# Stick-breaking attention on TensorE: an order written down and pinned, with units of a pair of heads between steps of the next pairs' projections

## The chip, the cores and the metric

The kernel runs on one core of one Trainium2 chip. The metric is device time in microseconds (us) of one execution. The engines named here are TensorE (PE, matrix products and transposes; PEld are its weight loads), VectorE (DVE), ScalarE (ACT), GpSimd (POOL) and SyncE (SP), whose queue issues the transfers between buffers.

## The reference, cut to what matters

A 512 x 1024 input goes through a first block (sparse attention and retention) and a second one: a feed-forward layer, a hybrid mixer, cross attention to a memory, a second feed-forward layer. All values are 32-bit floats. The change lies in the mixer's stick-breaking attention, of 16 heads of 64:

```python
proj = u @ w_in
q, k, v, z, xs, bm, cm, dt_raw = jnp.split(proj, np.cumsum(IN_SPLITS)[:-1], axis=-1)
...
for i in range(s_ // SB_BLOCK):                    # blocks of 128 rows
    z = jnp.einsum('bhtd,bhsd->bhts', qb, kb) * scale
    causal = s_idx[None, :] < t_idx[:, None]
    log_1mb = jnp.where(causal, jax.nn.log_sigmoid(-z), 0.0)
    suffix = lax.cumsum(log_1mb, axis=3, reverse=True) - log_1mb
    log_a = jnp.where(causal, jax.nn.log_sigmoid(z) + suffix, -jnp.inf)
    a = jnp.exp(log_a)
    outs.append(jnp.einsum('bhts,bhsd->bhtd', a, vb.astype(jnp.float32)))
```

With l = sigmoid(-z) and E the running product of l from the right, a weight is the difference of two neighbouring E, so the sum over a times v is a sum over E times the differences of neighbouring rows of v. That is the form in which the kernel computes it.

## The kernel before, in words

**Products.** A product of float32 is made of three in a faster format: each operand is split into a high part (ACT copies it) and a low part (DVE subtracts). A projection of 128 columns (`proj_T`, matmuls on line 164) takes 8 chunks of the 1024 inputs with 3 matmuls each, 24 in all, with 512 rows moving through. Its weights arrive by a transfer (`raw`, line 99) and are split into `whi` and `wlo` (lines 82 and 83).

**Pairs of heads.** The loop `for p in range(8)` takes two heads at a time, e = 0 and 1. Of each pair it projects q (24 matmuls), then k (24). The results are split into qh, ql and kh, kl, and SP copies them into the tiles Q, K0 and K1 (lines 1056 and 1059) that hold, for each head, the operand twice, one above the other, so that one matmul against K0 (high part of k) and one against K1 (low part) give the score in full precision. The copies of K are eight transfers of 64 rows: high and low part, upper and lower half (r), each for e = 0 and 1. Head e needs the two halves of K0 and of K1.

**Units.** A pair has three units (`GROUPS`): row blocks 0 and 1 together, row block 2, row block 3. For each unit and head there are scores (line 1070), their sigmoid `l` on ACT (line 1074), a running product `E` on DVE from right to left (`TENSOR_TENSOR_SCAN`, line 1079), transposes of E on PE (line 1087), and copies of them into `aT`: by ACT for e = 0, by DVE for e = 1 (lines 1094 and 1096). The values (line 1027) multiply `aT` by the differences `vv`; they are put off (`held`) by one unit, so the values of unit 0 stand behind the transposes of unit 1, and those of unit 2 behind the transposes of unit 0 of the next pair. Scores lie in two PSUM banks of the pool `s` and every third in bank 2 (`mm` in the trace); projections take banks 0 and 1; the transposes of e = 1 take bank 3 (`mm`), those of e = 0 the pool `tp`.

**Differences of v.** `vbefore` (lines 956 to 968) is v moved down by one row; DMAs fill it from `vv`, and DVE subtracts (line 967). Two buffers are taken in turn, so the DMAs of the third and fourth row block wait for the first and second subtraction. Behind it stand the projections of z, whose four PSUM banks per half are read by ACT and DVE (`ev_z`, lines 972 to 983).

**Order.** The program is written pair after pair, and a scheduler decides the order of the instructions on each engine by priorities and by costs of its own. On PE it mixes projections of the next pairs with units of this one. `after` adds waits by hand: the first transpose of a unit, and the first matmul of the values, wait for the last scan of that unit. What is marked by `tc.keep_in_program_order` is not reordered among what is marked; SP, ACT and DVE stay with the scheduler.

Of the kernel before, what the change touches and what calls it, by code (L numbers as in the profile page):

```python
# [18 lines left out]
NT = 4  # L19
# [12 lines left out]
def block_kernel(ctx, tc, A, out, upto=99):  # L32
# [161 lines left out]
    def proj_X(src, c0, w, get, consume, K=8, nt=NT, tail=1, kp=2, korder=None, between=None, slots=(), ready=None):  # L194

        banks = [bank() for _ in range(nt)]
        nch = (K + kp - 1) // kp
        ko = korder or list(range(K))

        def mms(t, ch, hl):  # L200
            for k in range(kp):
                kk = ch * kp + k
                if kk >= K:
                    continue
                xh, xl = get(ko[kk], t, t + 1)
                xh, xl = xh[:, 0, :], xl[:, 0, :]
                wh, wl = hl[0][:, k, :], hl[1][:, k, :]
                for n, (a, b) in enumerate(((xh, wh), (xl, wh), (xh, wl))):
                    PE.matmul(banks[t][:, :w], a, b, start=(kk == 0 and n == 0), stop=(kk == K - 1 and n == 2))  # L209
                    tick(w)  # L210
        for ch in range(nch - tail):
            hl = wload(src, ko[ch * kp], min(kp, K - ch * kp), c0, w)
            for t in range(nt):
                mms(t, ch, hl)
            if between:
                between(ch)
        slots = (None,) * (tail - len(slots)) + tuple(slots)
        last = ready or [(ch, wload(src, ko[ch * kp], min(kp, K - ch * kp), c0, w, slots[ch - nch])) for ch in range(nch - tail, nch)]
        for t in range(nt):
            for ch, hl in last:  # L220
                mms(t, ch, hl)
            consume(t, banks[t][:, :w])
        if between:
            between(nch - 1)
# [544 lines left out]
    def mixer(pair, st):  # L769
# [183 lines left out]
            return f  # L953
        for c in range(2):
            proj_X(w, 2048 + c * 512, 512, get, ev_v(c))
        vbefore = lambda t: d1.tile([128, D], F32, name="vbefore", tag=("xdt", "xdec")[t % 2])
        vb = vbefore(0)
        V.memset(vb[0:1], 0.0)
        for t in range(NT):
            nc.sync.dma_start(vb[1:113], vv[0:112, t])  # L960
            nc.sync.dma_start(vb[113:128], vv[112:127, t])
            nxt = None
            if t < NT - 1:
                nc.sync.dma_start(vl[t * 8 + 8:t * 8 + 16], vv[127:128, t].rearrange("o (p c) -> o p c", p=8))
                nxt = vbefore(t + 1)
                nc.sync.dma_start(nxt[0:1], vv[127:128, t])
            V.tensor_tensor(vv[:, t], vb, vv[:, t], op=ALU.subtract)
            vb = nxt


        zs = l1.tile([128, NT, D], F32, name="zs", tag="u3")
# [15 lines left out]
            return t[:, 0], t[:, 1]  # L987
        for g in range(2):
            proj_X(w, 3072 + g * 512, 512, get, ev_z(g), tail=2, slots=[spare])
        tp = tpp.tile([128, 4, 128], F32, name="tp")  # L990
        PE.transpose(tp[:, 0, 0:32], vl, ident[0:32, 0:32])
        vlT = l1.tile([128, NT, 8], F32, name="vlT")
# [24 lines left out]
        def values(p, segs, aTs, ob):  # L1017


            def f(*others):  # L1020

                pv = [(0, 0, 2, 0), (1, 1, 1, 2)] if len(segs) == 2 else [(segs[0][0], j, 1, j) for j in range(segs[0][0] + 1)]
                first = True
                for i, j, n, o in pv:
                    for e in range(2):
                        h = 2 * p + e
                        m = PE.matmul(ob[64 * e:64 * e + 64, i * 128:(i + n) * 128], vv[:, j, h * 64:(h + 1) * 64], aTs[e][:, o:o + n],  # L1027
                                      start=(i == 0), stop=(n == 2 or j == i), skip_group_check=True)
                        if first:
                            after(m, *others)  # L1030
                            first = False
                if segs is GROUPS[-1]:
                    for i in range(NT):
                        sl = slice(i * 128, (i + 1) * 128)
                        ACT.activation(oaF[:, p, sl], ob[:, sl], AF.Identity, bias=vlT[:, i, p:p + 1])
                    if p == 0:
                        ACT.activation(sq, oaF[:, p], AF.Square)
                    else:
                        q2 = a1.tile([128, 512], F32, name="q2")
                        ACT.activation(q2, oaF[:, p], AF.Square)  # L1040
                        V.tensor_tensor(sq, sq, q2, op=ALU.add)
            return f

        for p in range(8):

            Q = qk.tile([128, 2, 512], F32R, name="Q")
            K = [qk.tile([128, 2, 512], F32R, name=f"K{i}") for i in range(2)]
            for nm, c0, scale in (("q", 0, 0.125), ("k", 1024, None)):
                hi = a1.tile([128, 512], F32R, name=f"{nm}h")
                lo = a1.tile([128, 512], F32R, name=f"{nm}l")  # L1050
                proj_T(w, c0 + p * 128, 128, get, lambda j, bank, hi=hi, lo=lo, sc=scale: split(hi, lo, bank, sc), of=(0, 1))
                for r in range(2):
                    for e in range(2):
                        rows = slice(64 * e, 64 * e + 64)
                        if nm == "q":
                            nc.sync.dma_start(Q[64 * r:64 * r + 64, e].bitcast(F32), (hi, lo)[r][rows].bitcast(F32))
                        else:
                            for i, x in enumerate((hi, lo)):
                                nc.sync.dma_start(K[i][64 * r:64 * r + 64, e].bitcast(F32), x[rows].bitcast(F32))
            ob = None  # L1060
            for segs in GROUPS:
                T = segs[-1][1] + (segs[-1][0] + 1) * 128
                css, last = [], None
                for e in range(2):
                    sb = score_bank(p)
                    first = True
                    for i, off in segs:
                        W = (i + 1) * 128
                        for n, k in enumerate(K):
                            PE.matmul(sb[:, off:off + W], Q[:, e, i * 128:(i + 1) * 128], k[:, e, :W], start=first, stop=(n == 1),  # L1070
                                      skip_group_check=True)
                            first = False
                    l = a2.tile([128, 512], F32, name="l", bufs=3)
                    ACT.activation(l[:, :T], sb[:, :T], AF.Sigmoid, scale=-1.0)  # L1074

                    E = a2.tile([128, 512], F32, name="E", bufs=5)
                    for off, W in (((0, 128), (128, 256)) if len(segs) == 2 else ((0, T),)):
                        rev = slice(off + W - 1, (off - 1) if off else None, -1)
                        last = V.tensor_tensor_scan(E[:, rev], l[:, rev], own1[:, 511:(511 - W) if W < 512 else None:-1], 1.0,  # L1079
                                                    op0=ALU.mult, op1=ALU.max)  # L1080
                    css.append(E)

                aTs = []
                for e in range(2):
                    tp = tpp.tile([128, 4, 128], F32, name="tp") if e == 0 or p == 7 else bank((3,)).rearrange("p (j q) -> p j q", j=4)
                    for j in range(T // 128):
                        m = PE.transpose(tp[:, j], css[e][:, j * 128:(j + 1) * 128], ident)
                        if e + j == 0:
                            after(m, last)
                    aT = a2.tile([128, 4, 128], F32, name="aT", bufs=4)  # L1090

                    n = T // 128
                    own, rest = (slice(0, 3, 2), slice(1, 2)) if len(segs) == 2 else (slice(n - 1, n), slice(0, n - 1))
                    (V.tensor_copy if e else ACT.copy)(aT[:, rest], tp[:, rest])
                    if e:
                        V.tensor_scalar(aT[:, own], tp[:, own], -1.0, None, op0=ALU.add)
                    else:
                        ACT.activation(aT[:, own], tp[:, own], AF.Identity, bias=less1)
                    aTs.append(aT)
                if held:  # L1100
                    held.pop()(last)
                if ob is None:
                    ob = op_.tile([128, 512], F32, name="ob")
                held.append(values(p, segs, aTs, ob))
        held.pop()()
        osT = new_act()
        for t in range(NT):
# [199 lines left out]
```

## Time and profile before

| | |
|---|---|
| time, median of 3 runs | 1955.26 us (1954.87 to 1957.7) |
| profiled execution: time, span | 1953.41 us, 1951.6 us |
| PE busy | 1903.7 us, 98% |
| PEld busy | 1556.5 us, 80% |
| DVE busy | 982.8 us, 50% |
| ACT busy | 721.8 us, 37% |
| granted clock of TensorE, mean | 0.997 of full speed |

The span is the time from the first to the last instruction of the profiled execution, and all starts below are counted from its beginning. The stretch that the change touches runs from about 1133 us (first projection of q and k) to about 1313 us. Before it, from about 1095 us, v is shifted and z is projected. A row of the time line gives start, length, engine, line, operation, what is written from what is read, and in brackets how long the engine stood idle before and what ended that. Matmuls overlap: the next starts before the one before has ended.

### The profile page before, as it was taken

Reading aid. Unit: us, or ns where it says so; the run is one execution under the profiler, and the core shown is the slowest. Engines: PE = TensorE matmul, PEld = TensorE weight load, DVE = VectorE, ACT = ScalarE, POOL = GpSimd, SP = SyncE. Lnnn points to the kernel's source line nnn. Section 1 sums busy time; section 2 is a strip of 40 time slices with the busy share of each in tenths; the row PEclk is TensorE's granted clock in tenths of the full one; section 3 lists DMA queues with packets and bytes.
Section 4 is the critical chain, followed back from the end, with each engine's and each line's share of the span. In section 5 each row is a group of like instructions: output and inputs, shape, how many; then the busy total and the mean of one; then the engine's idle time right before and its main releaser. Section 6 shows DMA issues by size and latency. Waiting matters only on the chain.

```text
span 1951.6 us, 24228 instructions
## 1 busy us (share of the span) xinstructions
PE 1903.7 (98%) x9677; PEld 1556.5 (80%) x9677; DVE 982.8 (50%) x1681; ACT 721.8 (37%) x1246; POOL 38.3 (2%) x66
## 2 busy tenths in 40 slices
PE   7999999999999999999999999999999999999998
PEld 6778888788878888888877877767788888888887
DVE  5578833724553333324668755665464553333223
ACT  4345533233333323223445434544353432323221
POOL 0000000100000000000000000000000000000000
PEclk9999999999999999999999999999999999999999
DMA  7411133232332333333321445442262312333322
GB/s 245 130 44 34 34 97 97 87 98 86 108 97 87 98 97 97 98 97 119 89 82 50 128 121 136 128 120 76 87 194 78 105 57 86 97 98 97 97 97 86
DMA packets 154336, 193.21 MB, mean 99 GB/s; under 512 B 9976, under 2 KB 111732, under 8 KB 154096
## 3 DMA queue, kind: packets, MB, share of 16 engines
q1 hardware_dynamic: 154224, 191.66, 32.7%
q8 instruction: 76, 1.25, 0.3%
q14 instruction: 36, 0.29, 0.0%
HBM read 174.85 MB, written 2.10 MB: 91 GB/s over the span
## 4 chain that ended last, share of the span: by engine, by line
PE 84%; DVE 8%; ACT 1%; issue 1%; POOL 1%; DMA 1%; POOLq 0%; DVEq 0%; ACTq 0%
PE mm L164 43%; PE mm L209 27%; PE mm L187 3%; DVE E L1079 1%; DVE x_sb L279 1%; POOL rp_r L76 1%; PE ob L538 1%; DVE h L251 1%; PE ob L1027 1%; PE s L561 1%; PE ob L924 1%; PE s L1182 1%; PE s L1070 1%; DVE fg L272 1%; PE mm L579 1%
## 5 line engine op out<-in xcount | busy, mean ns | idle before, releaser
L83 DVE TENSOR_TENSOR wlo<-raw,whi 128x1024 fp32r<-128x1024 f32 (+1 forms) x274 | 333.6, 1218 | 680.3 <-ACT whi L82 675.0
L82 ACT ACTIVATE whi<-raw 128x1024 fp32r<-128x1024 f32 (+1 forms) x274 | 289.0, 1055 | 687.3 <-PE mm L164 289.9
L164 PE MATMUL mm<-a_hi,wlo 128*128 128x512 f32 x1120 | 438.0, 391 | 1.6 <-DVE wlo L83 1.6
L164 PE MATMUL mm<-a_hi,whi 128*128 128x512 f32 x1120 | 438.9, 392 | 0.0
L164 PE MATMUL mm<-a_lo,whi 128*128 128x512 f32 x1120 | 438.5, 392 | 0.0
L164 PEld LDWEIGHTS mm<-a_hi,wlo 128*128 128x128 f32 x1120 | 210.3, 188 | 44.5 <-DVE wlo L83 2.0
L164 PEld LDWEIGHTS mm<-a_lo,whi 128*128 128x128 f32 x1120 | 210.3, 188 | 44.0 <-issue 2.4
L164 PEld LDWEIGHTS mm<-a_hi,whi 128*128 128x128 f32 x1120 | 210.3, 188 | 43.3 <-issue 1.4
L209 PE MATMUL mm<-whi,a_hi 128*128 128x512 f32 (+1 forms) x384 | 151.2, 394 | 2.3 <-ACT a_hi L82 2.3
L209 PE MATMUL mm<-whi,a_lo 128*128 128x512 f32 (+1 forms) x384 | 151.7, 395 | 0.0
L209 PE MATMUL mm<-wlo,a_hi 128*128 128x512 f32 (+1 forms) x384 | 150.0, 391 | 0.0
L209 PE MATMUL mm<-whi,hid_hi 128*128 128x512 f32 x288 | 112.0, 389 | 0.0
L209 PE MATMUL mm<-whi,hid_lo 128*128 128x512 f32 x288 | 112.0, 389 | 0.0
L209 PE MATMUL mm<-wlo,hid_hi 128*128 128x512 f32 x288 | 112.0, 389 | 0.0
L209 PEld LDWEIGHTS mm<-whi,a_hi 128*128 128x128 f32 x384 | 72.9, 190 | 19.0 <-ACT a_hi L82 3.1
L209 PEld LDWEIGHTS mm<-whi,a_lo 128*128 128x128 f32 x384 | 72.9, 190 | 15.4 <-issue 2.5
L209 PEld LDWEIGHTS mm<-wlo,a_hi 128*128 128x128 f32 x384 | 72.8, 190 | 14.5 <-issue 1.8
L76 POOL TENSOR_TENSOR rp_r<-rp_a,half 128x1 f32<-128x1 f32 (+1 forms) x58 | 36.9, 636 | 1887.5 <-DVE rp_a L74 1565.0
L209 PEld LDWEIGHTS mm<-whi,hid_lo 128*128 128x128 f32 x288 | 54.1, 188 | 11.3
L209 PEld LDWEIGHTS mm<-wlo,hid_hi 128*128 128x128 f32 x288 | 54.1, 188 | 11.2
L209 PEld LDWEIGHTS mm<-whi,hid_hi 128*128 128x128 f32 x288 | 54.1, 188 | 11.2
L1079 DVE TENSOR_TENSOR_SCAN E<-l,own 128x128 f32<-128x128 f32 (+2 forms) x64 | 48.6, 809 | 10.9 <-ACT l L1074 10.9
(452 smaller groups left out, 2844.8 us busy)
## 6 DMA issues: line engine op xcount, KB each, us to landing
raw<-in_w_in_dram SPq DMA_DIRECT2D x96, 512.0 KB, 3.8
raw<-in_ffn_w_gu_dram SPq DMA_DIRECT2D x88, 512.0 KB, 3.6
raw<-in_ffn_w_down_dram SPq DMA_DIRECT2D x44, 512.0 KB, 3.7
raw<-in_w_out_dram SPq DMA_DIRECT2D x24, 512.0 KB, 3.7
raw<-in_xa_wkv_dram SPq DMA_DIRECT2D x16, 512.0 KB, 4.3
raw<-in_w_ret_o_dram SPq DMA_DIRECT2D x8, 512.0 KB, 3.4
K<-kh SPq DMA_DIRECT2D x32, 128.0 KB, 2.3
K<-kl SPq DMA_DIRECT2D x32, 128.0 KB, 2.3
```

Source lines behind the costliest of these rows:

```text
L76: POOL.tensor_tensor(r[:, :n], a[:, :n], half[:, :n], op=ALU.pow)
L82: ACT.activation(hi, src, AF.Copy)
L83: V.tensor_tensor(lo, src, hi.bitcast(F32), op=ALU.subtract)
L164: PE.matmul(o, a, b, start=(kc + k == 0 and n == 0 and si == 0), stop=(kc + k == K - 1 and n == 2), skip_group_check=True)
L187: PE.matmul(banks[g][j][:, t0 * 128:t1 * 128], a, b, start=(kc + k + n + si == 0), stop=(kc == 1 and k == 3 and n == 2), skip_group_check= ...
L209: PE.matmul(banks[t][:, :w], a, b, start=(kk == 0 and n == 0), stop=(kk == K - 1 and n == 2))
L251: V.scalar_tensor_tensor(h, src, r, g, op0=ALU.mult, op1=ALU.mult)
L272: V.tensor_tensor(fgt, bank, gpost[:, hf * 512:(hf + 1) * 512], op=ALU.mult)
L279: V.scalar_tensor_tensor(xs, fg[:, t if q == 0 else NT + t % 2], r, xs, op0=ALU.mult, op1=ALU.add)
L538: m = PE.matmul(ob[64 * e:64 * e + 64, a], vv[:, j, br, g * 64:(g + 1) * 64], pT[:, e, j], start=False, stop=(br == 1 and j == nk - 1), sk ...
L561: PE.matmul(sbs[e], qS[:, h, qsl], kk[:, br, g, :W], start=(n == 0 and (e == 0 or nk > 2)), stop=(n == 1), skip_group_check=True)
L1079: last = V.tensor_tensor_scan(E[:, rev], l[:, rev], own1[:, 511:(511 - W) if W < 512 else None:-1], 1.0, op0=ALU.mult, op1=ALU.max)
```

## The change

The two projections of each pair move into a generator, `projections()`, whose every step is one chunk (3 matmuls) of q or k. `steps(24)` runs the first 24 steps, that is q and k of pair 0 and q of pair 1. Then in each pair the units' scores, transposes and values stand in a written order with numbers of steps between them: 3 steps within the scores, 1 after the transposes of unit 0, 2 after those of unit 1 and its values, 10 after unit 2. So 16 steps fall in a pair p: the 8 of k of pair p+1, then the 8 of q of pair p+2. All these PE instructions are marked to keep that order, up to pair 6; pair 7 is left to the scheduler. The hand-made waits of `after` go where the order is pinned. The shift of v gets four buffers in place of two, all its DMAs are issued first, and the four subtractions stand behind the two halves of z.

```diff
-        vbefore = lambda t: d1.tile([128, D], F32, name="vbefore", tag=("xdt", "xdec")[t % 2])
-        vb = vbefore(0)
-        V.memset(vb[0:1], 0.0)
+        vb2 = d1.tile([128, 2, D], F32, name="vb2", tag="bcT")
+        vb = [d1.tile([128, D], F32, name="vb0", tag="xdt"), d1.tile([128, D], F32, name="vb1", tag="xdec"), vb2[:, 0], vb2[:, 1]]
+        V.memset(vb[0][0:1], 0.0)
...
-            V.tensor_tensor(vv[:, t], vb, vv[:, t], op=ALU.subtract)
-            vb = nxt
...
             proj_X(w, 3072 + g * 512, 512, get, ev_z(g), tail=2, slots=[spare])
+            for t in range(2 * g, 2 * g + 2):
+                V.tensor_tensor(vv[:, t], vb[t], vv[:, t], op=ALU.subtract)
...
+        def pe(m):
+            return tc.keep_in_program_order(m) if pinned[0] else m
+        QK = {}
+        def projections():
+            for p in range(8):
...
+                for nm, c0, scale in (("q", 0, 0.125), ("k", 1024, None)):
...
+                    for k in range(8):
+                        xh, xl = get(k, 0, NT)
+                        for n, (a, b) in enumerate(((wh, xh), (wh, xl), (wl, xh))):
+                            pe(PE.matmul(o, a[:, k], b, start=(k + n == 0), stop=(k == 7 and n == 2), skip_group_check=True))
+                        if k == 7:
+                            split(hi, lo, o, scale)
...
+                                        for i, x in enumerate((hi, lo)):
+                                            nc.sync.dma_start(K[i][64 * r:64 * r + 64, e].bitcast(F32), x[rows].bitcast(F32))
+                        yield
+        stream = projections()
+        def steps(n):
+            for _ in range(n):
+                next(stream, None)
...
+                for j in range(n):
+                    m = pe(PE.transpose(tp[:, j], Es[e][:, j * 128:(j + 1) * 128], ident))
+                    if e + j == 0 and not pinned[0]:
+                        after(m, last)
...
+        obs = [None]
+        steps(24)
         for p in range(8):
...
+            pinned[0] = p < 7
+            units = []
+            for u, segs in enumerate(GROUPS):
+                ES = []
                 for e in range(2):
...
+                    ES.append(score(p, segs, e))
+                    if u + e and (u, e) != (1, 0) and (u, e) != (0, 1) and p < 7:
+                        steps(1)
+                units.append((segs, [x for x, _ in ES], ES[1][1]))
+            for u, n in enumerate((1, 2, 10)):
+                turned(p, *units[u])
+                if p < 7:
+                    steps(n)
```

In the rows below, `mm<-a_hi,whi` and its like are the projections' matmuls, `s<-K,Q` and `mm<-K,Q` scores, `tp<-cst,E` and `mm<-cst,E` transposes, `ob<-aT,vv` values.

First, PE at the scores of the fourth pair. Before, 32 projection matmuls lie between the last one of that pair's k and the first score, which is the second row:

```order
L164 MATMUL mm_9802<-a_lo_6483,whi_9805 128x512
L1070 MATMUL s_9640<-K0_9556,Q_9555 128x128
L1070 MATMUL mm_9690<-K0_9556,Q_9555 128x384
L164 MATMUL mm_9802<-a_hi_6482,wlo_9806 128x512
L164 MATMUL mm_9802<-a_hi_6482,whi_9805 128x512
L1070 MATMUL s_9640<-K1_9557,Q_9555 128x128
L1070 MATMUL s_9640<-K0_9556,Q_9555 128x256
L1070 MATMUL s_9640<-K1_9557,Q_9555 128x256
L1070 MATMUL mm_9690<-K1_9557,Q_9555 128x384
L1070 MATMUL s_9650<-K0_9556,Q_9555 128x128
L164 MATMUL mm_9802<-a_lo_6483,whi_9805 128x512
L1070 MATMUL s_9697<-K0_9556,Q_9555 128x384
```

Two scores against K0 and two projection matmuls come before the first against K1, and further projection matmuls before the first score of head 1 (`s_9650`). Now the same place, with 24 projection matmuls between that pair's last of k and the first score:

```order
L1064 MATMUL mm_9650<-a_hi_6482,wlo_9647 128x512
L1091 MATMUL s_9681<-K0_9437,Q_9436 128x128
L1091 MATMUL s_9681<-K1_9438,Q_9436 128x128
L1091 MATMUL s_9681<-K0_9437,Q_9436 128x256
L1091 MATMUL s_9681<-K1_9438,Q_9436 128x256
L1091 MATMUL s_9691<-K0_9437,Q_9436 128x128
L1091 MATMUL s_9691<-K1_9438,Q_9436 128x128
L1091 MATMUL s_9691<-K0_9437,Q_9436 128x256
L1091 MATMUL s_9691<-K1_9438,Q_9436 128x256
L1091 MATMUL mm_9701<-K0_9437,Q_9436 128x384
L1091 MATMUL mm_9701<-K1_9438,Q_9436 128x384
```

K0 and K1 now alternate (`s_9681` is of head 0, `s_9691` of head 1), all scores of units 0 and 1 stand in one run, and eight projection matmuls fewer lie between k and the first of them.

Second, PE from the last score of that pair to the values of its unit 0. Before:

```order
L1070 MATMUL mm<-K_9556,Q 128x512
L1087 MATMUL tp<-cst,E 128x128 x3
L1087 MATMUL mm<-cst,E 128x128 x2
L1027 MATMUL ob<-aT,vv 64x128 x8
L1087 MATMUL tp<-cst,E 128x128 x3
L1070 MATMUL mm<-K_9557,Q 128x512
L1087 MATMUL mm<-cst,E 128x128 x3
L164 MATMUL mm<-a_hi,wlo 128x512
L164 MATMUL mm<-a_hi,whi 128x512
L1027 MATMUL ob<-aT,vv 64x256 x2
```

Now the same stretch:

```order
L1091 MATMUL mm<-K_9438,Q 128x512
L1064 MATMUL mm<-a_hi,whi 128x512
L1064 MATMUL mm<-a_lo,whi 128x512
L1064 MATMUL mm<-a_hi,wlo 128x512
L1113 MATMUL tp<-cst,E 128x128 x3
L1113 MATMUL mm<-cst,E 128x128 x3
L1025 MATMUL ob<-aT,vv 64x128 x8
L1064 MATMUL mm<-a_hi,whi 128x512
L1064 MATMUL mm<-a_lo,whi 128x512
L1064 MATMUL mm<-a_hi,wlo 128x512
L1113 MATMUL tp<-cst,E 128x128 x3
L1113 MATMUL mm<-cst,E 128x128 x3
```

The last score now comes before any transpose, and three projection matmuls stand on each side of the transposes of unit 0 and their values.

Third, PE where the projections of q and k begin, behind those of z. Before, the first five matmuls are of k (one bank), then q follows in another:

```order
L991 MATMUL tp_8940<-cst_88,vl_8332 128x32
L164 MATMUL mm_9007<-a_hi_6482,whi_9010 128x512
L164 MATMUL mm_9007<-a_lo_6483,whi_9010 128x512
L164 MATMUL mm_9007<-a_hi_6482,wlo_9011 128x512
L164 MATMUL mm_9007<-a_hi_6482,whi_9010 128x512
L164 MATMUL mm_9007<-a_lo_6483,whi_9010 128x512
L164 MATMUL mm_8968<-a_hi_6482,whi_8971 128x512
```

Now q is first, whole, and its bank is the one that held z's fourth row block:

```order
L989 MATMUL tp_8939<-cst_88,vl_8332 128x32
L1064 MATMUL mm_8973<-a_hi_6482,whi_8969 128x512
L1064 MATMUL mm_8973<-a_lo_6483,whi_8969 128x512
L1064 MATMUL mm_8973<-a_hi_6482,wlo_8970 128x512
L1064 MATMUL mm_8973<-a_hi_6482,whi_8969 128x512
```

The first matmul of q now waits for the read of that bank by DVE (line 977 before, 973 after), for which before only the sixth matmul waited. On SP, ACT and DVE the order around k and its scores is as before: whi, kh, whi, qh, then the six `l` on ACT; wlo, kl, wlo, ql, then the eight scans on DVE; the eight copies of K, then those of Q on SP.

## Rows read from the trace of the kernel before

**Rows 1.** The page, part 4: the chain that ended last, by engine.

```profile
PE 84%; DVE 8%; ACT 1%; issue 1%; POOL 1%; DMA 1%; POOLq 0%; DVEq 0%; ACTq 0%
```

**Rows 2.** Waits of PE from 1130 to 1330: total us, times, longest.

```profile
PE mm L1087 <- DVE aT L1096: 5.8, 7, 0.9
PE mm L236 <- DVE kl L83: 2.3, 1, 2.3
```

**Rows 3.** Time line of PE, third pair: start, length, what, idle before.

```profile
1187.12 0.39 PE L164 MATMUL mm<-a_hi,wlo 128*128 128x512 f32 x1
1187.35 0.40 PE L164 MATMUL mm<-a_hi,whi 128*128 128x512 f32 x1
...
1194.40 0.39 PE L164 MATMUL mm<-a_lo,whi 128*128 128x512 f32 x1
1194.62 0.22 PE L1070 MATMUL s<-K,Q 128*128 128x128 f32 x1
...
1198.06 0.74 PE L1070 MATMUL s<-K,Q 128*128 128x512 f32 x2
...
1199.80 1.09 PE L1027 MATMUL ob<-aT,vv 128*64 128x128 f32 x16
1200.90 0.52 PE L1087 MATMUL tp<-cst,E 128*128 128x128 f32 x3
1201.17 0.47 PE L1070 MATMUL mm<-K,Q 128*128 128x512 f32 x1
1202.52 0.41 PE L1087 MATMUL mm<-cst,E 128*128 128x128 f32 x2 [0.88 <-DVE aT L1096]
```

**Rows 4.** Time line of PE: first projections behind the values of pairs 0, 2, 6.

```profile
1165.17 0.50 PE L164 MATMUL mm<-a_hi,whi 128*128 128x512 f32 x1
...
1207.51 0.50 PE L164 MATMUL mm<-a_lo,whi 128*128 128x512 f32 x1
...
1290.48 0.50 PE L164 MATMUL mm<-a_lo,whi 128*128 128x512 f32 x1
1290.82 0.40 PE L164 MATMUL mm<-a_hi,wlo 128*128 128x512 f32 x1
```

**Rows 5.** Time line of ACT: the high part of the third pair's k.

```profile
1188.29 0.58 ACT L82 ACTIVATE kh<-mm 128x512 fp32r<-128x512 f32 x1
```

**Rows 6.** Time line of DVE: the low part of the same k.

```profile
1189.56 0.68 DVE L83 TENSOR_TENSOR kl<-mm,kh 128x512 fp32r<-128x512 f32 x1
```

**Rows 7.** Time line of SP's queue: five of the eight copies of that k.

```profile
1190.27 1.10 SPq L1059 DMA_DIRECT2D K<-kl  x2
1191.42 0.60 SPq L1059 DMA_DIRECT2D K<-kh  x1
1192.06 0.60 SPq L1059 DMA_DIRECT2D K<-kl  x1
...
1193.56 0.58 SPq L1059 DMA_DIRECT2D K<-kl  x1
```

**Rows 8.** The page, part 6: size, median us from issue to landing.

```profile
K<-kl SPq DMA_DIRECT2D x32, 128.0 KB, 2.3
```

**Rows 9.** Time line of PE behind the projections of z.

```profile
1132.94 0.24 PE L991 MATMUL tp<-cst,vl 32*128 32x32 f32 x1
...
1135.43 0.50 PE L164 MATMUL mm<-a_hi,wlo 128*128 128x512 f32 x1 [1.57 <-DVE wlo L83]
```

**Rows 10.** Time line of DVE: the read of z's fourth bank.

```profile
1135.29 0.68 DVE L977 SCALAR_TENSOR_TENSOR zs<-zs,mm 128x512 f32<-128x512 f32 x1
```

**Rows 11.** Stretches: busy us of PE, PEld, DVE, ACT, POOL, then granted clock, DMA.

```profile
1133.10:1136.50 3.40, 1.83 (x8) 1.19 (x8) 3.37 (x7) 1.27 (x3) 0.32 (x1) 1.00 0.01 2
1339.00:1342.50 3.50, 1.58 (x7) 0.96 (x7) 3.50 (x6) 1.65 (x3) 0.00 (x0) 1.00 0.00 0
1342.50:1346.00 3.50, 3.50 (x10) 2.73 (x9) 1.39 (x2) 0.00 (x0) 0.00 (x0) 0.51 0.63 184
```

**Rows 12.** Line 967, the subtractions of v: count, min/median/max ns, first and last.

```profile
L967 DVE TENSOR_TENSOR vv<-vbefore,vv x4: 1217/1218/1220, 1096.5 to 1112.8; 128x1024 f32<-128x1024 f32 x4
```

More of the change, by code (lines that the diff above doesn't have):

```diff
@@ L955, in mixer @@
             proj_X(w, 2048 + c * 512, 512, get, ev_v(c))
-        vbefore = lambda t: d1.tile([128, D], F32, name="vbefore", tag=("xdt", "xdec")[t % 2])
-        vb = vbefore(0)
-        V.memset(vb[0:1], 0.0)
+        vb2 = d1.tile([128, 2, D], F32, name="vb2", tag="bcT")
+        vb = [d1.tile([128, D], F32, name="vb0", tag="xdt"), d1.tile([128, D], F32, name="vb1", tag="xdec"), vb2[:, 0], vb2[:, 1]]
+        V.memset(vb[0][0:1], 0.0)
         for t in range(NT):
-            nc.sync.dma_start(vb[1:113], vv[0:112, t])
-            nc.sync.dma_start(vb[113:128], vv[112:127, t])
-            nxt = None
+            nc.sync.dma_start(vb[t][1:113], vv[0:112, t])
+            nc.sync.dma_start(vb[t][113:128], vv[112:127, t])
             if t < NT - 1:
                 nc.sync.dma_start(vl[t * 8 + 8:t * 8 + 16], vv[127:128, t].rearrange("o (p c) -> o p c", p=8))
-                nxt = vbefore(t + 1)
-                nc.sync.dma_start(nxt[0:1], vv[127:128, t])
-            V.tensor_tensor(vv[:, t], vb, vv[:, t], op=ALU.subtract)
-            vb = nxt
+                nc.sync.dma_start(vb[t + 1][0:1], vv[127:128, t])
         zs = l1.tile([128, NT, D], F32, name="zs", tag="u3")
@@ L1026, in f @@
                         h = 2 * p + e
-                        m = PE.matmul(ob[64 * e:64 * e + 64, i * 128:(i + n) * 128], vv[:, j, h * 64:(h + 1) * 64], aTs[e][:, o:o + n],
-                                      start=(i == 0), stop=(n == 2 or j == i), skip_group_check=True)
+                        m = pe(PE.matmul(ob[64 * e:64 * e + 64, i * 128:(i + n) * 128], vv[:, j, h * 64:(h + 1) * 64], aTs[e][:, o:o + n],
+                                         start=(i == 0), stop=(n == 2 or j == i), skip_group_check=True))
                         if first:
@@ L1042, in values @@
             return f
-        for p in range(8):
[L1046 to L1063, printed above, removed]
-                for e in range(2):
[L1065 to L1104, printed above, removed]
@@ new lines, in mixer @@
+        pinned = [True]
+        def pe(m):
[3 more added lines that the diff above has]
+            for p in range(8):
+                Q = qk.tile([128, 2, 512], F32R, name="Q")
+                K = [qk.tile([128, 2, 512], F32R, name=f"K{i}") for i in range(2)]
+                QK[p] = Q, K
+                for nm, c0, scale in (("q", 0, 0.125), ("k", 1024, None)):
+                    hi = a1.tile([128, 512], F32R, name=f"{nm}h")
+                    lo = a1.tile([128, 512], F32R, name=f"{nm}l")
+                    wh, wl = wload(w, 0, 8, c0 + p * 128, 128)
+                    o = bank((0, 1))
+                    for k in range(8):
[4 more added lines that the diff above has]
+                            split(hi, lo, o, scale)
+                            for r in range(2):
+                                for e in range(2):
+                                    rows = slice(64 * e, 64 * e + 64)
+                                    if nm == "q":
+                                        nc.sync.dma_start(Q[64 * r:64 * r + 64, e].bitcast(F32), (hi, lo)[r][rows].bitcast(F32))
+                                    else:
+                                        for i, x in enumerate((hi, lo)):
+                                            nc.sync.dma_start(K[i][64 * r:64 * r + 64, e].bitcast(F32), x[rows].bitcast(F32))
+                        yield
@@ new lines, in mixer, with score @@
+        stream = projections()
+        def steps(n):
+            for _ in range(n):
+                next(stream, None)
+        def score(p, segs, e):
+            Q, K = QK[p]
+            T = segs[-1][1] + (segs[-1][0] + 1) * 128
+            sb = score_bank(p)
+            first = True
+            for i, off in segs:
+                W = (i + 1) * 128
+                for n, k in enumerate(K):
+                    pe(PE.matmul(sb[:, off:off + W], Q[:, e, i * 128:(i + 1) * 128], k[:, e, :W], start=first, stop=(n == 1),
+                                 skip_group_check=True))
+                    first = False
+            l = a2.tile([128, 512], F32, name="l", bufs=3)
+            ACT.activation(l[:, :T], sb[:, :T], AF.Sigmoid, scale=-1.0)
+            E = a2.tile([128, 512], F32, name="E", bufs=5)
+            for off, W in (((0, 128), (128, 256)) if len(segs) == 2 else ((0, T),)):
+                rev = slice(off + W - 1, (off - 1) if off else None, -1)
+                last = V.tensor_tensor_scan(E[:, rev], l[:, rev], own1[:, 511:(511 - W) if W < 512 else None:-1], 1.0,
+                                            op0=ALU.mult, op1=ALU.max)
+            return E, last
@@ new lines, in turned @@
+        def turned(p, segs, Es, last):
+            n = segs[-1][1] // 128 + segs[-1][0] + 1
+            own, rest = (slice(0, 3, 2), slice(1, 2)) if len(segs) == 2 else (slice(n - 1, n), slice(0, n - 1))
+            aTs = []
+            for e in range(2):
+                tp = tpp.tile([128, 4, 128], F32, name="tp") if e == 0 or p == 7 else bank((3,)).rearrange("p (j q) -> p j q", j=4)
+                for j in range(n):
+                    m = pe(PE.transpose(tp[:, j], Es[e][:, j * 128:(j + 1) * 128], ident))
+                    if e + j == 0 and not pinned[0]:
+                        after(m, last)
+                aT = a2.tile([128, 4, 128], F32, name="aT", bufs=4)
+                (V.tensor_copy if e else ACT.copy)(aT[:, rest], tp[:, rest])
+                if e:
+                    V.tensor_scalar(aT[:, own], tp[:, own], -1.0, None, op0=ALU.add)
+                else:
+                    ACT.activation(aT[:, own], tp[:, own], AF.Identity, bias=less1)
+                aTs.append(aT)
+            if held:
+                held.pop()(*(() if pinned[0] else (last,)))
+            if segs is GROUPS[0]:
+                obs[0] = op_.tile([128, 512], F32, name="ob")
+            held.append(values(p, segs, aTs, obs[0]))
```

## The prediction, written before the changed kernel was run

> **What bounds the kernel now.** I read the chain of work that ended last, then the waits of PE in the stretch of the change, then the time lines of PE, ACT, DVE and SP over one pair of heads. PE carries 84% of the chain [rows 1]; the transfers carry 1%, but that does not make them harmless, as the SP rows will show. In the stretch the waits of PE are few: seven times the transposes of E wait for the DVE copies into `aT`, 5.8 us together, and once, at the end, 2.3 us for the low part of the last k [rows 2]. A pair of heads repeats: from pair 2 to pair 6 the first projection matmul behind a pair's values moves from 1207.51 to 1290.48 [rows 4], so a pair takes 82.97 / 4 = 20.74 us.
>
> How much of that is waiting? Projection matmuls follow each other every (1194.40 - 1187.35) / 31 = 0.2274 us [rows 3]. Two losses show in the rows. The last score of unit 2 starts at 1201.17 and would be through 0.23 later; the next transpose starts at 1202.52, so 1.12 us is lost per pair. And from the first score, 1194.62, to the end of the two at 1198.06 (3.89 us) lie seven projection matmuls (1.59) and scores of 4096 columns (at 512 columns per 0.2274 us, 1.82): 0.48 is lost. Without both a pair would take 19.1 us. That is the upper bound of a pair without waits; the lower one, 18.4, takes off a third loss of about 0.7 us that I estimate at the many changes between kinds of matmul, which no row shows singly. I use the middle, 18.75.
>
> **What the change takes away.** With the last score ahead of all transposes and three projection matmuls on each side of the transposes of unit 0, most of those 2 us can be covered. If nothing else became late, a pair would take 18.75 in place of 20.74.
>
> **What becomes late: the copies of K.** This is the step that decides. The third pair's k ends with the matmul at 1187.12 [rows 3]. ACT writes kh until 1188.87 [rows 5], DVE kl until 1190.24 [rows 6]. SP then issues the copies one behind the other, the sixth (K1, head 0) at 1192.06, the eighth (K1, head 1) at 1193.56 [rows 7], and one lands 2.3 us behind its issue [rows 8]. So K1 is there for head 0 7.24 us, and for head 1 8.74 us, behind the last matmul of k. Before, 32 projection matmuls lie between, so the first score is 7.5 us behind k, and the scheduler put K0 first and seven projections among the scores. Now 24 lie between: the first score is due 25 x 0.2274 = 5.69 us behind k, and K1 of head 1 is wanted after head 0's 768 columns and one score of 128, 0.40 later, at 6.09. PE is pinned, so nothing can step in: it stands still 8.74 - 6.09 = 2.65 us in all, in four pieces. Bounds: nothing, if the landing times of the median hide faster ones; 2.65 if this pair is typical; 3.8 if the landing is as late as the order before could bear (7.5 + 0.4 + 2.0 of projections and scores ahead of head 1). I take 2.6, which is the row.
>
> Queued behind the wait on PE is everything, since it is the engine that sets the end; ACT's `l` and the eight scans on DVE start later by the same amount, so they are not late in addition. A pair then takes 18.75 + 2.6 = 21.35 us against 20.74. From the values of pair 0 to those of pair 6 that is 6 x 21.35 = 128.1, against 1290.48 - 1165.17 = 125.3 [rows 4]: **+2.8**.
>
> A rule of the Trainium skill bears on this: "DMA: Bandwidth & Descriptors", section "Anatomy of one DMA — SWDGE (gpsimd) path", puts a fixed cost of about 2.0 us on a transfer, nearly all of it completion, and only about 50 ns on the sequencer's dispatch. The 2.3 us to landing agrees; the dispatch does not, for SP's issues take 0.58 to 0.60 us each here [rows 7]. By the page's price all eight copies would be out 0.4 us after kl, the last would land about 5.8 us behind k, ahead of its use, and the time would be that of the first rival below.
>
> **The head.** PE ends z's products and a small transpose at 1132.94 + 0.24 = 1133.18 [rows 9]. Before, two matmuls ran then and the third waited 1.57 us for weights. Now the first matmul of q needs the bank that DVE reads until 1135.29 + 0.68 = 1135.97 [rows 10], so PE starts at about 1136.0, after 2.8 us idle. Pair 0's k ends with the 48th matmul, 1136.0 + 47 x 0.2274 = 1146.7; K1 of head 1 is there at 1155.4. From there to the end of the pair's values lies the pair's 18.75 less 6.09 (k to that use) and less 1.5 (six projections that stand behind the values): 11.2. Pair 0 lacks the eight values of a pair before it, 1200.90 - 1199.80 = 1.1 us [rows 3], so it ends at 1165.5, against 1165.17: **+0.3**.
>
> **The clock.** An idle TensorE is granted less. 1.57 us of idling at 1133.9 left the clock at 1.00; a stretch of 3.5 us in which PE was busy 1.58 was followed by 3.5 us at 0.51, its lower level of 1.2 GHz [rows 11]. The idling of 2.8 us at the new head is longer than both, so I count one such fall: 3.5 x (1 - 0.51) = **+1.7**. Bounds: 0 and, if it lasts twice as long, 3.4.
>
> **The tail.** Pair 7's k now has six matmuls behind the values of pair 6 in place of two [rows 4]: 4 x 0.2274 = **+0.9**. The 2.3 us wait for its kl [rows 2] stays.
>
> **The shift of v.** Four subtractions of 1.22 us [rows 12] move on DVE and no wait of PE names them; their transfers are issued sooner, and the transfers of weights issued behind them have slack in the z projections: 0. If that cover were gone, it would be at most one transfer's delay, about 2 us.
>
> **The sum.** 2.8 + 0.3 + 1.7 + 0.9 = +5.7. On the profiled execution, 1953.41, that is 1959.1; its time lies 1.85 below the median of the runs, so on the median, 1955.26, it is 1961.0. Errors of 0.4 us in a pair make 2.5, the clock term 1.7: likeliest range 1956 to 1966.
>
> **The rivals.**
> - *The copies of K are not waited for* (they land sooner than the rows say): a pair takes 18.75 to 19.9, the second if the wait of 1.12 for `aT` stays, because the copies stand behind all eight scans on DVE. Six pairs give 112.5 to 119.4 in place of 125.3; the head gains 2.6 too. With clock and tail: -12.5 to -5.6, so about 1946. For it: the idle of 0.88 that the waits name would go. Against it: rows 5 to 8, and the pinned 24.
> - *Half of the wait*: it is 1.3 a pair, seven times, 9.1 less than forecast: -3.4, 1952, no change that can be told. For it: the landing time is a median of 32 copies, and a single one may be faster.
> - *The clock falls in every pair*: the wait for K leaves PE idle for 2.6 of about 3 us, with single scores between, seven times. If each costs 1.7 like the fall that rows 11 show: 7 x 1.7 = 11.9 more, 1973, slower without doubt. It decides as soon as two pairs show it. For it: 1.58 busy in 3.5 brought the fall. Against it: 1.83 busy in 3.4 did not [rows 11], and four pieces of idling are not one. The Trainium skill, "TensorE: Matmul & The Clock Gate", section "A second HAM failure mode: psum-queue depth-cycling", tells of a kernel whose short idle times between groups of matmuls made the clock swing. The trace of before, with an idle 0.88 in each pair, does not show that; by that rule this rival would be the forecast.
> - That the order is not what the change says can be ruled out: it stands in PE's instructions.
>
> **How the numbers follow.** A difference under 0.2%, 3.9 us, can hardly be told from none; "same" is 1951.4 to 1959.2. Forecast 0.50, of which 0.16 falls under 1959.2 and the rest is slower. K not waited for 0.20, of which 0.02 same. Half of the wait 0.12, of which 0.02 faster. Clock in every pair 0.18, slower. Together faster 0.20, same 0.28, slower 0.52. The range leaves out about half of the first rival and half of the last: 1946 to 1973.
>
> **What would show it.** Right: PE's waits before the scores name the copies of K (or SP), about 2.6 us in each of pairs 0 to 6; pairs lie 21.3 apart; the first matmul of q starts at about 1136.0 and is followed by a stretch at a clock near 0.5; the waits for `aT` are gone. Wrong: pairs under 20 us apart with the first score 5.7 us behind k, which is the first rival; a granted clock well below 1 between 1150 and 1290, which is the last; or transposes that wait over 0.5 us for scans or copies in each pair.

## The result, and the profile after

The changed kernel takes 1968.63 us (median of 4, 1966.26 to 1969.53) against 1955.88 us on the same chip: ratio 1.0062, 95% interval 1.0045 to 1.0080, so 9 to 16 us slower. The profiled spans differ by 1967.7 - 1951.6 = 16.1 us. Forecast were 1961, slower, likeliest 1956 to 1966, with a range of 1946 to 1973.

Where the 16.1 us lie is read from the first projection matmul behind the values of a pair. The time line of PE, at pairs 0 to 6 (to be set against [rows 4]):

```profile
1169.86 0.50 PE L1064 MATMUL mm<-a_hi,whi 128*128 128x512 f32 x1
...
1192.86 0.50 PE L1064 MATMUL mm<-a_hi,whi 128*128 128x512 f32 x1
...
1214.70 0.50 PE L1064 MATMUL mm<-a_hi,whi 128*128 128x512 f32 x1
...
1237.87 0.50 PE L1064 MATMUL mm<-a_hi,whi 128*128 128x512 f32 x1
...
1259.23 0.50 PE L1064 MATMUL mm<-a_hi,whi 128*128 128x512 f32 x1
...
1282.23 0.50 PE L1064 MATMUL mm<-a_hi,whi 128*128 128x512 f32 x1
...
1306.05 0.50 PE L1064 MATMUL mm<-a_hi,whi 128*128 128x512 f32 x1
```

Pair 0 ends 4.7 us later than before (0.4 of it is there already at the transpose behind z, ahead of the changed part), from the end of pair 0 to that of pair 6 it takes 136.2 us against 125.3 (+10.9), and the rest, 1967.7 - 1306.05 = 661.7 against 661.1, is nearly as before. A pair takes 21.4 to 21.8 us twice and 23.0 to 23.8 otherwise: there are two kinds. The waits of PE from 1166 to 1290 (us, times, longest; against [rows 2]):

```profile
PE s L1091 <- DMA K<-kl: 3.5, 10, 0.6
PE s L1091 <- DMA K<-kh: 2.7, 3, 1.0
PE s L1091 <- issue: 2.0, 3, 0.9
```

The wait for `aT` is gone there and the scores wait for the copies of K. The time line of PE at the third pair, whose k ends with the matmul at 1194.12 (against [rows 3]):

```profile
1194.12 0.39 PE L1064 MATMUL mm<-a_hi,wlo 128*128 128x512 f32 x1
...
1199.56 0.39 PE L1064 MATMUL mm<-a_hi,wlo 128*128 128x512 f32 x1
1200.82 0.33 PE L1091 MATMUL s<-K,Q 128*128 128x128 f32 x1 [0.87 <-DMA K<-kh]
1201.40 0.61 PE L1091 MATMUL s<-K,Q 128*128 128x128 f32 x3 [0.26 <-DMA K<-kl]
1202.24 0.30 PE L1091 MATMUL s<-K,Q 128*128 128x128 f32 x1 [0.23 <-issue]
1203.16 0.59 PE L1091 MATMUL s<-K,Q 128*128 128x128 f32 x3 [0.62 <-DMA K<-kl]
```

The queue of SP for the same k (against [rows 7]):

```profile
1195.89 1.11 SPq L1074 DMA_DIRECT2D K<-kh  x2
1197.27 1.11 SPq L1074 DMA_DIRECT2D K<-kl  x2
1198.42 0.60 SPq L1074 DMA_DIRECT2D K<-kh  x1
1199.07 0.60 SPq L1074 DMA_DIRECT2D K<-kl  x1
1199.70 0.60 SPq L1074 DMA_DIRECT2D K<-kh  x1
1200.66 0.47 SPq L1074 DMA_DIRECT2D K<-kl  x1
```

Four idle pieces, each ending some 2.3 to 2.5 us behind the issue of one of the last four copies: 1198.42, 1199.07, 1199.70 and 1200.66 against 1200.82, 1201.40, 1202.24 and 1203.16. PE goes on 9.04 us behind k. At the head, behind z's products, PE waits as forecast (against [rows 9]; line 74 is the instruction behind the read of the bank on DVE):

```profile
1133.30 0.25 PE L989 MATMUL tp<-cst,vl 32*128 32x32 f32 x1
1136.38 0.78 PE L1064 MATMUL mm<-a_hi,whi 128*128 128x512 f32 x1 [2.83 <-DVE rp_a L74]
```

Now the clock, in stretches of 3.4 us at the head and at pairs 0 to 6 (columns as in [rows 11]; the clock is the third number from the end):

```profile
1136.40:1139.80 3.40, 3.40 (x8) 2.75 (x9) 2.33 (x8) 2.00 (x3) 1.50 (x2) 0.50 0.56 154
1156.90:1160.30 3.40, 3.25 (x10) 2.91 (x11) 2.78 (x6) 1.90 (x4) 0.00 (x0) 0.50 0.78 170
1180.90:1184.30 3.40, 3.40 (x9) 2.73 (x9) 2.97 (x5) 1.46 (x4) 0.00 (x0) 0.51 0.88 224
1203.00:1206.40 3.40, 3.24 (x17) 2.87 (x18) 2.68 (x6) 1.85 (x4) 0.00 (x0) 1.00 0.81 188
1225.50:1228.90 3.40, 3.40 (x11) 2.91 (x11) 2.70 (x4) 1.48 (x4) 0.00 (x0) 0.55 0.85 218
1248.00:1251.40 3.40, 3.40 (x19) 2.94 (x18) 3.18 (x6) 1.92 (x5) 0.00 (x0) 1.00 0.77 185
1269.80:1273.20 3.40, 3.40 (x11) 2.95 (x10) 2.96 (x5) 1.47 (x3) 0.00 (x0) 0.53 0.86 231
1293.60:1297.00 3.40, 3.40 (x10) 2.90 (x10) 3.20 (x6) 1.45 (x3) 0.00 (x0) 0.52 0.78 249
```

The clock falls to its lower level behind the head and behind the wait for K in pairs 0, 1, 3, 5 and 6, not in 2 and 4: these are the two short pairs. A fall costs 3.4 x 0.5 = 1.7 us.

How long PE idled does not tell the two kinds apart. The four pieces of the third pair, above, come to 1.98 us, and no fall followed; ahead of the scores of pair 0, where one did, the time line names only these:

```profile
1155.74 0.30 PE L1091 MATMUL s<-K,Q 128*128 128x128 f32 x1 [1.13 <-DMA K<-kh]
1156.21 2.19 PE L1091 MATMUL s<-K,Q 128*128 128x128 f32 x7 [0.18 <-DMA K<-kl]
```

### The profile page after: what moved, and what is told of

It is laid out like the page before. It is cut to its first block, busy times and chain, and to the rows that moved or that the text cites. A ratio compares the mean times of both kernels' runs of the same rounds, so it can differ in the third digit from the quotient of the medians.

```text
span 1967.7 us, 24243 instructions
## 1 busy us (share of the span) xinstructions
PE 1911.2 (97%) x9677; PEld 1567.2 (80%) x9677; DVE 983.6 (50%) x1681; ACT 724.9 (37%) x1246; POOL 38.6 (2%) x66
## 4 chain that ended last, share of the span: by engine, by line
PE 83%; DVE 7%; DMA 2%; POOL 1%; issue 1%; ACT 1%; SPq 1%; POOLq 0%; DVEq 0%; ACTq 0%
PE mm L164 38%; PE mm L209 27%; PE mm L1064 4%; PE mm L187 3%; DVE x_sb L279 1%; POOL rp_r L76 1%; PE ob L538 1%; PE ob L1025 1%; SPq L1074 1%; DMA K<-kl 1%; DVE h L251 1%; PE s L561 1%; PE ob L924 1%; PE s L1091 1%; PE s L1221 1%
## 5 line engine op out<-in xcount | busy, mean ns | idle before, releaser
L164 PE MATMUL mm<-a_hi,wlo 128*128 128x512 f32 x992 | 387.4, 391 | 0.0
L164 PE MATMUL mm<-a_lo,whi 128*128 128x512 f32 x992 | 387.0, 390 | 0.0
L164 PEld LDWEIGHTS mm<-a_hi,whi 128*128 128x128 f32 x992 | 186.3, 188 | 39.4 <-issue 1.2
L164 PEld LDWEIGHTS mm<-a_hi,wlo 128*128 128x128 f32 x992 | 186.3, 188 | 38.5 <-issue 0.2
L164 PEld LDWEIGHTS mm<-a_lo,whi 128*128 128x128 f32 x992 | 186.3, 188 | 37.5 <-issue 0.3
```

Source lines behind the costliest of these rows:

```text
L164: PE.matmul(o, a, b, start=(kc + k == 0 and n == 0 and si == 0), stop=(kc + k == K - 1 and n == 2), skip_group_check=True)
```

## The experiments

Theory: PE waits for K's copies because too few projections stand between k and its scores, and the clock falls behind that wait. Rivals: the pinned order is bad in itself; the shift of v costs; the falls have another cause. Each row of the table gives the median, the ratio to the kernel before on the same chip with its 95% interval, and how far apart the ends of pairs 0 to 4 lie (in the kernel before 20.7 us, the first 21.6). The runs stand on several chips, so two runs are compared by their ratios.

| run | us | ratio (interval) | pair, us |
|---|---|---|---|
| changed kernel | 1968.63 | 1.0062 (1.0045 to 1.0080) | 21.4 to 23.2 |
| 26 steps | 1946.65 | 0.9960 (0.9949 to 0.9972) | 19.4 |
| 28 steps | 1948.55 | 0.9966 (0.9952 to 0.9980) | 19.15 |
| other bank first | 1965.85 | 1.0064 (1.0049 to 1.0080) | 21.4 to 23.3 |
| 12 fillers | 1965.97 | 1.0067 (1.0049 to 1.0085) | 21.86 |
| 9 fillers | 1962.53 | 1.0035 (1.0019 to 1.0052) | 21.4 to 21.8 |
| shift of v alone | 1957.02 | 1.0004 (0.9991 to 1.0017) | 20.7 (first 21.6) |
| kh from ACT's queue | 1999.86 | 1.0228 (1.0205 to 1.0250) | 25.0 to 27.1 |
| nothing pinned | 1959.79 | 1.0018 (1.0005 to 1.0030) | 21.4 (first 20.7) |
| 26 steps, other bank | 1942.11 | 0.9934 (0.9914 to 0.9954) | 19.4 |
| 27 steps, other bank | 1942.07 | 0.9926 (0.9906 to 0.9947) | 19.15 |
| 28 steps, other bank | 1943.77 | 0.9946 (0.9927 to 0.9964) | 19.14 |
| 29 steps, other bank | 1958.01 | 1.0010 (0.9998 to 1.0021) | 20.9 (first 22.5) |

**More steps ahead.** One number changes; every pair's k then ends that many steps earlier.

```diff
-        steps(24)
+        steps(28)
```

> Only the first number of steps changes, 24 to 28: 36 projection matmuls lie between a pair's k and its first score, 24 before. Theory (PE waits for the copies of K, and the clock falls behind that wait): the first score is due 8.4 us behind k, the last copy is wanted at 8.8 and there at 8.74, so no wait; pairs 18.8 to 19.3 us apart, clock 1.0 from 1150 to 1290; about 1945 us. Rival (the pinned order is itself worse, because scans and transposes stand in a run): pairs stay at 21 to 23 us, 1966 to 1971. Rival (landing follows k's place and is late again because q's copies come first in SP's queue): a wait of over 1 us stays, about 1957.

> 24 to 26 steps: 30 projection matmuls between k and the first score. Theory: half of the wait goes, 1.3 us a pair stays, pairs about 20.0 us, and a shorter wait brings fewer falls of the clock (none to two): 1953 to 1957. Rival (a threshold, the wait goes or stays as a whole): the same as with 24 or with 28. Rival (the pinned order is itself worse): 1966 to 1971.

With 28 the waits of PE from 1150 to 1285 hold none for K, and at the fourth pair the first eight scores run in one piece (waits, then the stretch of one pair, then the time line):

```profile
PE mm L1113 <- DVE aT L1119: 1.6, 2, 1.2
PE mm L1113 <- DVE rp_a L74: 0.9, 1, 0.9
```

```profile
1191.59:1210.72 19.13, 19.13 (x123) 15.41 (x121) 11.98 (x20) 9.58 (x21) 0.00 (x0) 1.00 0.57 142
```

```profile
1217.44 0.39 PE L1064 MATMUL mm<-a_hi,wlo 128*128 128x512 f32 x1
1217.67 1.08 PE L1091 MATMUL s<-K,Q 128*128 128x128 f32 x8
```

PE is busy for the whole pair, at full clock. So the pinned order is not bad in itself: it is the distance from k to its scores. With 26 the expected 1.3 us of wait did not stay (19.4, not 20.0): I had left out that the transposes and values now between k and the scores also take time. At the fourth pair the first score starts 8.9 us behind the last matmul of k with 26 steps (1216.82 - 1207.88) and 12.1 with 28 (1217.67 - 1205.52), not after the 7.0 and 8.4 that the projections alone take. Both beat the kernel before, by 0.4 and 0.3%; 28 was forecast some 3.5 us faster than it was.

**The wait filled.** Matmuls whose result the score overwrites, ahead of the first score:

```diff
             first = True
+            if p < 7 and e == 0 and segs is GROUPS[0]:
+                xh, _ = get(0, 0, NT)
+                for _ in range(12):
+                    pe(PE.matmul(sb, get(0, 0, 1)[0][:, 0, :], xh, start=True, stop=True, skip_group_check=True))
```

> Ahead of the first score of pairs 0 to 6 stand 12 more matmuls of 512 columns (2.73 us), whose result is thrown away by the score that follows in the same bank. Theory: they run within the wait for K (2.6 us), so a pair still takes about 21.4 us, but PE does not idle and the clock stays at 1.0 from 1150 to 1290; the five falls of 1.5 us go: about 1961. Rival (the falls have nothing to do with the idling): clock as in the changed kernel, 1969 to 1970. Rival (there is no true wait of that size, the trace misplaces it): 7 x 2.73 us more, about 1985.

> As the run with 12 thrown-away matmuls ahead of the first score, but 9 (2.05 us). With 12, pairs took 21.86 us, 0.5 more than the 21.37 that a pair without a fall takes: too many by 2. Theory: 9 fit into the wait, pairs 21.4 us, and PE idles so little that the clock stays at 1.0 in the pairs: 7 x 0.5 = 3.4 less than with 12, 1962 to 1963. Rival (what the 12 cost is not their number but the switch into them): 1965 to 1966.

The stretch of the pairs with 12:

```profile
1150.00:1290.00 140.00, 138.23 (x813) 111.71 (x812) 76.85 (x120) 61.57 (x129) 1.10 (x2) 1.00 0.55 137
```

and in the changed kernel itself:

```profile
1150.00:1290.00 140.00, 128.61 (x725) 101.39 (x723) 76.51 (x118) 60.76 (x128) 1.10 (x2) 0.95 0.52 132
```

84 useless matmuls leave the time where it was (ratio 1.0067 against 1.0062), and the clock stays at 1.00 in the pairs: the wait is true, and the falls come from idling. I had said 1961 for 12 and it was 1965.97: a pair takes 21.86, which is what the longer of the two pairs without a fall took (21.84) and 0.5 more than the shorter (21.36). With 9 it is 1962.53, as expected, at the same clock (1.00); that the number was met is in part luck, since of the 4.3 us between the profiled runs with 12 and with 9 only 1.1 lie between the ends of pairs 0 and 6, and 1.5 arose ahead of the changed part.

**The head.** The banks in the other order.

```diff
         obs = [None]
+        turn[(0, 1)] += 1
```

> The two banks of the projections are taken in the other order, so that the first q does not need the bank that z's fourth row block leaves last. Theory: the first matmul of q starts about 1133.5 in place of 1136.4 and the fall of the clock behind that idling goes: 2.9 + 1.5 = 4.4 us less, about 1964. Rival (the head is hidden by the wait for the copies of pair 0's K): under 1 us less, 1968.

The 2.8 us of idling and the fall behind it are gone. PE goes on right behind the small transpose, which starts at 1134.23 here, at full clock (time line, then stretch):

```profile
1134.41 0.50 PE L1064 MATMUL mm<-a_hi,whi 128*128 128x512 f32 x1
```

```profile
1134.40:1137.80 3.40, 3.40 (x16) 2.80 (x16) 3.37 (x7) 1.26 (x3) 0.35 (x1) 1.00 0.01 2
```

Counted from that transpose, pair 0 ends after 31.2 us, against 36.6 in the changed kernel, so the rival is wrong in the trace; 1.4 us of it are lost again up to the end of pair 6. Alone the time does not show it: the ratio is the same, with intervals of 3 us each way. On top of 26 and 28 steps the ratios fall by what is 5.1 and 3.9 us, near the 4.5 forecast, but the intervals overlap, so neither gain is sure by itself.

> 26 steps ahead and the banks in the other order: both repairs that worked alone. Theory (they add up): 1946.65 less the idling at the head and its fall of the clock, 2.8 + 1.7 = 4.5: 1942. Rival (the head's gain is taken back where the copies of pair 0's K are waited for): 1946.

> 28 steps ahead and the banks in the other order. Theory: pairs 19.15 us apart as with 28 alone, head without idling or a fall: 1948.55 - 4.5 = 1944. Compared with 26 steps: less wait per pair, but the projections run out two steps earlier in pair 6, so more is left uncovered at the end. Rival (no gain at the head): 1948.

> 27 steps ahead, banks in the other order. Theory: 33 projection matmuls between k and the first score, which is then due 7.7 us behind k, the last copy wanted at 8.1 and there at 8.74: pairs about 19.2 us, 1942 to 1944, between 26 and 28 steps. Rival (what follows the pairs decides: transposes and weights behind pair 7 fall differently for each number): anything from 1938 to 1947.

26 and 27 steps are the fastest, 0.7% below the kernel before, and cannot be told apart from each other, nor surely from 28.

> 29 steps ahead, banks in the other order. Theory: the copies of K are early with 27 already, so pairs stay at 19.1 us and only the end changes, where the projections run out one step earlier in pair 6 than with 28: 1942 to 1946. Rival (q's and k's results come so early that Q's buffer of the pair before is waited for): pairs over 19.3 us, over 1947.

With 29 the gain is gone, by neither of my reasons. Waits of PE from 1150 to 1290:

```profile
PE mm L1113 <- DVE aT L1119: 10.8, 6, 2.1
```

and DVE in pair 0:

```profile
1157.80 4.02 DVE L1100 TENSOR_TENSOR_SCAN E<-l,own 128x384 f32<-128x384 f32 x4
1161.73 1.20 DVE L83 TENSOR_TENSOR wlo<-raw,whi 128x1024 fp32r<-128x1024 f32 x1
1162.85 0.68 DVE L83 TENSOR_TENSOR kl<-mm,kh 128x512 fp32r<-128x512 f32 x1
1163.45 0.28 DVE L1117 COPY aT<-mm 128x128 f32<-128x128 f32 x1
1163.65 0.42 DVE L1119 TENSOR_SCALAR aT<-mm 128x256 f32<-128x256 f32 x1
```

k now ends so early that its split and that of the weights behind it, 1.9 us of DVE, stand ahead of the copies into `aT`, and the transposes wait for those. With 28 steps and the other bank the first copies into `aT` of pair 0 (1158.72) still stand ahead of both splits (from 1159.23).

**The copies from two queues.** The copies of kh go to ACT's queue.

```diff
-                                            nc.sync.dma_start(K[i]
+                                            (nc.sync if i else nc.scalar).dma_start(K[i]
```

> The changed kernel with the four copies of kh issued by ScalarE's queue, those of kl by SyncE's as before; order on TensorE unchanged. Theory (the copies are late because one queue issues eight of them, 0.6 us each): the last of K0 is out 3.6 us behind k and lands at 5.9, the last of K1 is out at 5.0 and lands at 7.3, so 1.2 us of wait stay per pair in place of 2.6, and fewer falls of the clock: 1950 to 1957. Rival (landing itself is the delay, whoever issues): 1966 to 1970. Rival (issuing costs ScalarE so much that qh and the sigmoids come late): slower than 1970.

31 us slower than the changed kernel, and not for my third reason: PE waits for the copies of K. SP's queue at the third pair, then the median from issue to landing of both kinds:

```profile
1203.26 0.37 SPq L99 DMA_DIRECT2D raw<-in_w_in_dram  x1
1203.86 3.27 SPq L1074 DMA_DIRECT2D K<-kl  x4
```

```profile
K<-kh ACTq DMA_DIRECT2D x32, 128.0 KB, 2.6
K<-kl SPq DMA_DIRECT2D x32, 128.0 KB, 5.6
```

The scheduler now sends a load of weights (512 KB) ahead of the copies of kl, which land 5.6 us behind their issue in place of 2.3. It is not a matter of SP's queue alone. Of two neighbouring copies of kh on ACT's queue, issued at 1202.99 and 1203.65, with the load of 1203.26 between them, the first and the second landed after:

```profile
DMA to landing us min/median/max: 2.6/2.6/2.6
DMA to landing us min/median/max: 5.2/5.2/5.2
```

So the run does not test whether the rate of issues is to blame; it shows what a large load issued just before does to the copies, whichever queue issues them. The granted clock is lower too, 0.984 on average against 0.992. The changed kernel has such a load once: it goes out ahead of pair 6's K, whose copies then land after up to 3.6 us, and the first score waits 2.2 us.

**The rest of the change.** The shift of v in the kernel before; and the changed program with `pinned = [False]`.

> The kernel before with the shift of v alone changed (four buffers, subtractions behind the halves of z). Theory (it is hidden): 1954 to 1957, no difference. Rival (its transfers push the weights of z back): 2 to 3 us slower, 1958, and the projections of z end later than in the kernel before.

> The changed program with nothing pinned: generator, steps and shift of v stay, and the scheduler is free to order TensorE's instructions again, with the waits made by hand back in place. Theory (the loss is the pinned place of k, not the rewriting): the scheduler puts about 33 projection matmuls between k and the scores, as before the change; pairs 20.7 us, no falls of the clock in the pairs: 1954 to 1958. Rival (the rewriting, by other buffers or the order of allocation, costs as well): over 1960.

The shift of v costs nothing that can be measured, and the projections of z do not end later for it: from ACT's last copy of v (1086.10 before, 1088.55 here) to the transpose behind z (1132.94 and 1135.41) it is 46.8 and 46.9 us. With nothing pinned the scheduler goes back to the old distance and no copy of K is waited for, but it puts the last score ahead of the transposes; the wait for `aT` grows from 5.8 us in all to 7.9 in six pairs (from 1166 to 1290):

```profile
PE mm L1113 <- DVE aT L1119: 7.9, 6, 1.5
```

That is 1959.79, 3.5 us (1.0 to 5.9) slower than before: a small part of the rewriting costs by itself, which I had not expected. The wait for `aT` is not all of it. In the profiled run 2.2 us lie between the ends of pairs 0 and 6, and 2.8 at the head, where pair 0 ends 35.0 us behind the transpose behind z, 32.2 before. There PE idles 1.57 us for weights as it did before, when the clock stayed at 1.00; here it fell (stretch from 1138.4):

```profile
1138.40:1141.80 3.40, 3.40 (x10) 2.69 (x9) 2.33 (x10) 2.01 (x3) 1.51 (x2) 0.55 0.54 154
```

## Why the prediction was right or wrong

The direction and the wait for K were right. The time lies above the likeliest range and inside the stated one, which reaches it only because half of the rival "the clock falls in every pair" was counted in.

- *The copies of K are late*: right. The last score of the four waits ended 9.04 us behind k, forecast 8.74; pairs without a fall of the clock took 21.84 and 21.36 us, forecast 21.35. That the second is met so closely is luck, as the next point shows. Moving k (26, 28 steps) takes the wait away.
- *A pair without waits, 18.75*: 19.15, measured with 28 steps, which is the upper bound that two losses gave; of the third, estimated at the changes between kinds of matmul, nothing was to be had. Against 19.15 the wait for K cost 2.2 and 2.7 us in the two pairs without a fall, forecast 2.6: in the shorter one the pair was forecast 0.4 too short and the wait 0.4 too long.
- *The head*: the idling was as forecast (2.83 us, then 3.4 us at half clock). Pair 0 ended 4.7 us later against 2.0 forecast: its own fall (1.7), a start of q that was 0.4 later, because the profiled run was that much later already ahead of the change, and 0.6 us of wait for `aT` at its second unit.
- *The clock*: the term that was mis-sized. I counted one fall, at the head, and gave the fall in every pair a chance of 0.18. There were six, five of them behind the wait for K: 5 x 1.7 = 8.5 us. 1961 + 8.5 is 1969.5; measured 1968.63. On the profiled runs the same sum, 5.7 + 8.5 = 14.2, is 1.9 short of 16.1, so the closeness of the first is in part luck. "Four pieces of idling are not one" was the wrong reason: idling in two or three pieces, 1.3 to 2.4 us together, did bring the fall in five pairs of seven, and its size does not decide, since 2.0 and 1.5 us in the other two, in four and three pieces, brought none. Nor does the 1.57 us at the head, which left the clock at 1.00 in the kernel before but not with nothing pinned. The Trainium skill, "TensorE: Matmul & The Clock Gate", section "A second HAM failure mode: psum-queue depth-cycling", tells of a kernel, one that cycles through PSUM banks, in which short idle times between groups of matmuls made the clock swing. This trace agrees as to the swing, with clocks of 0.50 to 0.55 behind five such waits and 1.00 behind two, though its idling comes from transfers. What decides between them is open.
- *Tail and shift of v*: +0.5 us for the part behind pair 6 against +0.9; nothing for the shift, as said.
- *The price of an issue*: the section of the Trainium skill that the prediction sets beside SP's issues, "Anatomy of one DMA — SWDGE (gpsimd) path" of "DMA: Bandwidth & Descriptors", is on transfers that GpSimd issues. No copy of K or Q goes that way here, so the 0.46 to 0.60 us of an issue on SP neither bear out nor refute its 50 ns.

## What to carry to other kernels

When an order is pinned, the distance from a producer's last matmul to the first use has to cover the whole way, split and copies included; here that way is 8.7 to 9 us and 24 matmuls of 0.23 us do not cover it, while the 8.9 us with 26 steps do. A short stall on TensorE is to be counted with the half clock that may follow: the wait for K cost 2.2 to 2.7 us in a pair without a fall and 3.8 to 4.0 with one (23.0 to 23.2 against 19.15, pairs 1, 3 and 5). Shift the phase of such a pipeline by one number and measure both sides: 26 to 28 are good, 24 and 29 are not, for different reasons.

## What the runs showed that I had not expected

In the changed kernel a fall of the clock lasted 3.4 us each time at the head and in the pairs, and the same wait brought it in some pairs and not in others. It is not always 3.4: behind the wait for pair 7's kl it lasted 6.8 us, before the change as after it, and with 26 steps the one at the head did. The kernel before, from 1294.6:

```profile
1294.60:1301.40 6.80, 6.11 (x23) 4.94 (x23) 2.77 (x4) 2.39 (x4) 0.00 (x0) 0.51 0.75 203
```

A copy of 64 rows lands 2.3 us behind its issue, but 5 to 7 us behind it when a 512 KB load was sent just before it, from the same queue or from another.
